# Seven products of quarters for two column groups of the values projection, mixed with the stationary projections, with linear attention behind them

## The chip, the cores and the metric

The kernel runs on one core of one Trainium2 chip. The metric is the device time of one execution in microseconds; the median of several runs is compared. TensorE (PE in the profile) multiplies matrices into PSUM, an accumulator memory of eight banks of 512 float32 columns on 128 partitions. VectorE (DVE) and ScalarE (ACT) do the elementwise work, GpSimd (POOL) and SyncE (SP) mostly issue transfers. Each engine works through its own queue in order; semaphores make one wait for another.

## The reference

Two layers, each on 256 tokens of width 2048. All projections of a layer come from the same input `x` (256 x 2048):

```python
h = x @ w_in                      # a_q, a_k, a_v, a_z, b_q, b_k, b_v, b_z, b_lr, m_q, m_z
y_a = chunk_band_attention(a_q, a_k, a_v, rel_table)     # 8 heads of 128
log_g = log_sigmoid(b_lr @ gate_w + gate_b) / GATE_TAU   # b_lr: 16 columns
o_b = gla_chunk_recurrence(b_q, b_k, b_v, log_g)         # gated linear attention, 4 heads
y_b = rms_norm(o_b) * gla_norm_g
mk, mv = split(mem @ w_mem_kv)
y_m = memory_attention(m_q, mk, mv)                      # 4 heads, 256 memory tokens
y = concat(y_a * silu(a_z), y_b * silu(b_z), y_m * silu(m_z))
x = layer_norm(alpha * x + y @ w_out, ln_g, ln_b)
```

The change touches the values: the product of `x` with the columns of `b_lr`, `b_v` and `a_v`, 16 + 512 + 1024 = 1552 columns in all.

## The kernel before

**Arithmetic.** Every big product is done in three matmuls of a 32-bit format of TensorE: each operand is split into a high part (a cast, on ACT) and a low part (operand minus high part, on DVE), and high x high, low x high and high x low are accumulated. For activations the split is done once and kept (`xq[l]`, four operands of four k tiles each); for weights it is done for each piece as it arrives.

**Weights as a stream of pieces.** `plan()` writes out the order in which all pieces of weights are used (`loads`). A piece is 128 partitions x 1024 columns (512 KB) for most products and 128 x 776 (two k tiles of 388 columns, 388 KB) for the values. `take()` hands out the next piece and lets `advance()` issue what lies ahead of it: the transfer into a ring of four raw tiles (`RAWS`) on SP's queue, the cast three pieces ahead (`high`, line 200, ACT), the low part two pieces ahead (`low`, line 207, DVE). The order of PE and SP is the order in which the program issues; ACT and DVE are put in an order by the scheduler of the framework, where these casts and low parts go first (`tc.high_priority(AHEAD)`).

**Two kinds of projection.** In a stationary projection (`ws_group`) the weights are the stationary operand and the output is transposed, features on partitions; 512 columns of output take two halves of four pieces, each half into two PSUM banks (`pair()` gives banks 0 and 1 or 2 and 3 in turn). In a moving projection (`as_group`) a 128 x 128 block of `x` is stationary and the weights stream through: 388 columns of values in eight pieces of 12 matmuls (two k tiles, two halves of the tokens, three products). `values(i)` does the i-th of four such groups and copies the result into `asv` (tokens on partitions).

**The order in a layer.** Memory keys and values first (16 pieces; in layer 1, `norm_between` prepares that layer's `xq` behind them). Then BQK (linear attention's queries and keys), `values(0)`, `values(1)`, `values(2)`, AQ0, AK0, `values(3)`, AQ1, AK1, MQ, the four gates BZ, AZ0, AZ1, MZ, and the output projection. All but the values and the output are stationary projections of eight pieces.

**Background work by ticks.** Linear attention (`gla`), the attention heads (`a_head`, eight), the memory heads (`m_head`, four), `norm_between` and `norm_residual` are generators that wait in a list. After each piece the program calls `tick()`: at most two generators are active, and at most one of them, in turns, is advanced by one step; the number that it yields says how many ticks it rests. So the few matmuls of a step come into PE's queue between two pieces of a projection, and its DVE and ACT work runs beside the pieces that follow. `banks(n)` takes banks from a list `free` (4 to 7 from `values(2)` on). `gla` needs `values(0)` and `values(1)` (its gates, its values), so it starts at `values(2)`; the heads 0 to 3 are put into the list when `values(2)`, AQ0 and AK0 are done. Where the result of generators is needed, `finish(gens)` calls `tick()` until they are done:

```python
sz = gated()
total(sz, a, b)
act.activation(sz, sz, AF.Silu)
finish(gens[i])
dve.tensor_tensor(yraw[i][:, j:j + 2], sz, yraw[i][:, j:j + 2], op=ALU.mult)
```

This stands at the end of each half of a gate: BZ needs linear attention (`gens[0]`), AZ0 the heads 0 to 3, AZ1 the heads 4 to 7, MZ the memory heads.

Of the kernel before, what the change touches and what calls it, by code (L numbers as in the profile page):

```python
# [16 lines left out]
P = 128  # L17
# [10 lines left out]
VISITS = ((-1, 0), (1, 2), (3, 4), (5,))  # L28

# [7 lines left out]
class Load:  # L37
    def __init__(self, src, shape, home=None, quarter=None):
        self.src, self.shape, self.home, self.quarter = src, shape, home, quarter
        self.raw = self.hi = self.lo = self.room = None  # L40


@with_exitstack
def hybrid_trunk_kernel(
# [81 lines left out]
    xq = [[] for _ in range(L)]  # L126

    def plan():
        for l in range(L):
# [14 lines left out]
            for p in range(8):  # L144
                if l == 0 and p < 4:
                    loads.append(Load(xT[p], (4, T), "res", (xq[l], p)))
                loads.append(Load(w512[l, G_BQK, p], (4, 256)))
            for i in range(4):
                group(w388[l, i], 2, 388)
                for g in ((), (), (G_AQ0, G_AK0), (G_AQ1, G_AK1))[i]:  # L150
                    loads.extend(Load(w512[l, g, p], (4, 256)) for p in range(8))
            for g in (G_MQ, G_BZ, G_AZ0, G_AZ1, G_MZ):
                loads.extend(Load(w512[l, g, p], (4, 256)) for p in range(8))
# [12 lines left out]
    rooms = []  # L166
# [6 lines left out]
    def start_load(d):  # L173
        kp, n = d.shape
        if d.home == "res":
# [13 lines left out]
    def high(d):  # L189
# [9 lines left out]
        with tc.high_priority(AHEAD):  # L199
            act.copy(d.hi, d.raw)  # L200
# [10 lines left out]
    def raws(i):  # L211
        return sum(1 for d in loads[at["lo"]:i] if d.home != "res" and not d.room)

    def advance(hi, lo):
        def dma(upto):
            while at["dma"] < min(upto, len(loads)):
                if loads[at["dma"]].home != "res" and not loads[at["dma"]].room and raws(at["dma"]) >= RAWS:
                    return
                start_load(loads[at["dma"]])
                at["dma"] += 1  # L220
# [83 lines left out]
    def ws_group(l, after=None, first=None):  # L304
        for half in range(2):
            a = pair() if half or first is None else first
            for p in range(4):
# [5 lines left out]
                if p == 3:  # L313
                    v = ps[:, a:a + 2].rearrange("p b (h t) -> p b h t", h=2)
                    yield half * 2, v[:, :, 0], v[:, :, 1]
                tick()

# [38 lines left out]
    def gla_inputs(l):  # L356
        gb = small([P, 2], "gb")
        ng = small([P, 1], "ng")
        raw = small([P, 256], "gws")
# [8 lines left out]
    def gla(gb, ng, gq, gk, asv, yraw):  # L368
# [29 lines left out]
        b_ = hd.tile([P, 512], F32, name=nm("b"), tag="gb_")  # L398
# [28 lines left out]
        qe = hd.tile([P, 512], F32, name=nm("qe"), tag="qe")  # L427
# [217 lines left out]
    def norm_between(x):  # L645
# [13 lines left out]
        for q in range(4):  # L659
            o = operand()  # L660
            x.append(o)
            for j in range(0, 4, 2):
# [10 lines left out]
                parts(o[:, j:j + 2, 0], o[:, j:j + 2, 1], z)  # L673
                yield 2 if (q, j) == (2, 2) else 1

    def norm_residual(rows):
        for n, (g, b) in enumerate(rows):
            for t in range(2):
                r = res[:, t, columns(n)]
                dve.tensor_tensor(r, r, g, op=ALU.mult)  # L680
                dve.tensor_tensor(r, r, b, op=ALU.add)
                yield 1
# [43 lines left out]
    gens, rows = [], None  # L726
    for l in range(L):
# [28 lines left out]
        if l:  # L756
            finish(gens)
            waiting.append(norm_residual(rows))

        yraw = [per.tile([P, 4, T], F32, name=nm("yr"), tag=f"yr{i}") for i in range(4)]  # L760
# [6 lines left out]
        for i, a, b in ws_group(l, None, 4):  # L767
            total(gk if i else gq, a, b, 1.0 if i else 0.125)
        gp = gla_inputs(l)
        if l == 0:  # L770
# [8 lines left out]
            sp.dma_start(res, xn.rearrange("(t p) d -> p t d", p=P))  # L779

        asv = per.tile([P, 2, 1552], F32, name=nm("asv"), tag="asv")

        def values(i):
            for acc in as_group(xq[l], 388):
                act.copy(asv[:, :, i * 388:(i + 1) * 388], acc)

        def heads():
            t = hd.tile([P, 4, T], F32, name=nm("qk"), tag="qk", bufs=4)
            for i, a, b in ws_group(l):
                total(t[:, i:i + 2], a, b)  # L790
            return t

        values(0)
        values(1)
        if l == 0:
            pe.transpose(ps[:, 7, :P], lng, ident)
            act.copy(lnt, ps[:, 7, :32].rearrange("p (a k) -> p a k", a=2))
        free[:] = [4, 5, 6, 7]
        bias = {}
# [4 lines left out]

        load_bias(0)
# [3 lines left out]
        for half in range(2):  # L809
            values(2 + half)  # L810
            q, k = heads(), heads()
            gens.append([a_head(half * 4 + h, load_bias, bias, q[:, h], k[:, h], asv, yraw[1 + half][:, h]) for h in range(4)])
            waiting.extend(gens[-1])
        q = [hd.tile([P, 4, T], F32R, name=nm("mq"), tag="qk", bufs=4) for _ in range(2)]
        for i, a, b in ws_group(l):
            tmp = gated()
            total(tmp, a, b)
            parts(q[0][:, i:i + 2], q[1][:, i:i + 2], tmp)
        gens.append([m_head(h, q, mk, mv, yraw[3][:, h]) for h in range(4)])
# [15 lines left out]
        for i in range(4):  # L835
            for j, a, b in ws_group(l, cut_y if i == 3 else None):
# [10 lines left out]
        rows = gain_rows(l)  # L847
        if last:
            gbrow = per.tile([2, 1024], F32, name="gbrow", tag="yr0")
# [9 lines left out]
        if not last:  # L859
            gens = [norm_between(xq[l + 1])]  # L860
# [112 lines left out]
```

## Time and profile before

| | |
|---|---|
| time, median of 3 runs | 929.47 us (929.41 to 930.95) |
| profiled execution: time and span | 930.37 us, 928.6 us |
| busy: PE, DVE, ACT | 920.9, 592.7, 503.7 us |
| mean granted clock of TensorE | 0.998 |
| moved by DMA | 178.79 MB, 193 GB/s in the mean |
| layer 0: `values(2)` from, `gla`'s last transposes, last memory head's transposes | about 108.5, 200, 344 us |

The busy time of PE counts matmuls, whose ends are modelled; it says that PE has work, not at which rate. Rows of groups read: line, engine, operation, output<-inputs, shape, count | busy time in us, mean ns of one | idle time of the engine before them and what ended it. Rows of the timeline read: start in us, duration in us, engine, line, operation; several like instructions in sequence are one row. A line can be that of a helper: line 77 issues nearly all matmuls, lines 337 and 338 copy an accumulator out, lines 341 and 342 split an activation, 520 to 539 are the end of `gla`, 596 to 610 are in `m_head`, 839 is a gate's SiLU. Rows of stretches read: stretch, its length, busy time of PE, of PE's weight loads, of DVE, ACT and POOL (with counts), granted clock, DMA share, GB/s.

### The profile page before, as it was taken

The page shows a single profiled execution, that of the slowest core. Times are in us where ns is not written, and L with a number is a line of the kernel's source. Part 1 is how long each engine was busy: PE and PEld are TensorE (multiplying, and loading weights), DVE is VectorE, ACT ScalarE, POOL GpSimd, SP SyncE. Part 2 cuts the span into 40 slices and gives each one's busy share as a digit, 9 for nine tenths or more (in the row PEclk, how much of TensorE's full clock was granted, in tenths as well). Part 3 has the DMA queues.
Part 4 walks back from the last instruction along what each step waited for, and adds up shares of the span by engine and source line. Part 5 has one row for each costly group of instructions (what it writes and reads, how often), then busy time and mean ns, then how long its engine had stood idle before and what let it go on. Part 6 is the DMA issues. An engine that isn't in the chain of part 4 may idle for free.

```text
span 928.6 us, 14327 instructions
## 1 busy us (share of the span) xinstructions
PE 920.9 (99%) x5558; PEld 808.5 (87%) x5558; DVE 592.7 (64%) x789; ACT 503.7 (54%) x727; POOL 17.6 (2%) x40
## 2 busy tenths in 40 slices
PE   9999999999999999999999999999999999999997
PEld 6889998898888888888888899889988888888875
DVE  6574497665566666555589544965655666666566
ACT  6563584484456665443468446746644566563340
POOL 2000000000000000000000000000000000100000
PEclk9999999999999999999999999999999999999999
DMA  8867765465645467555665566655655455665552
GB/s 283 291 216 266 213 211 166 149 188 178 196 162 170 170 194 225 195 197 189 201 230 189 171 185 202 186 180 153 201 179 182 163 172 182 216 200 196 190 174 90
DMA packets 58580, 178.79 MB, mean 193 GB/s; under 512 B 6416, under 2 KB 9616, under 8 KB 58256
## 3 DMA queue, kind: packets, MB, share of 16 engines
q1 hardware_dynamic: 56560, 173.05, 57.4%
q0 software_dynamic: 1664, 4.31, 2.0%
q8 instruction: 43, 0.70, 0.3%
q10 hardware_dynamic: 288, 0.52, 0.2%
q14 instruction: 25, 0.20, 0.1%
HBM read 175.76 MB, written 2.10 MB: 192 GB/s over the span
## 4 chain that ended last, share of the span: by engine, by line
PE 96%; DMA 1%; DVE 1%; SPq 1%; issue 0%; ACT 0%; ACTq 0%; DVEq 0%
PE ps L77 95%; DMA raw<-w 1%; DMA room<-w 1%; DVE wl L207 1%; PE ps L572 1%; PE ps L668 0%; PE ps L610 0%; SPq L272 0%; PE ps L539 0%; SPq L267 0%; ACT res L700 0%; DVE w L207 0%; ACT wh L200 0%; PE ps L441 0%; SPq L179 0%
## 5 line engine op out<-in xcount | busy, mean ns | idle before, releaser
L207 DVE TENSOR_TENSOR wl<-raw,wh 128x1024 fp32r<-128x1024 f32 (+1 forms) x313 | 365.7, 1170 | 262.2 <-PE ps L77 207.2
L200 ACT CAST wh<-raw 128x1024 fp32r<-128x1024 f32 (+1 forms) x313 | 314.8, 1007 | 327.4 <-PE ps L77 228.7
L77 PE MATMUL ps<-x,wh 128*128 128x512 f32 x1408 | 448.8, 400 | 0.0
L77 PEld LDWEIGHTS ps<-x,wl 128*128 128x128 f32 x1408 | 264.3, 188 | 63.3 <-DVE wl L207 1.2
L77 PE MATMUL ps<-wh,x 128*128 128x512 f32 (+1 forms) x1112 | 319.0, 368 | 0.1
L77 PE MATMUL ps<-x,wl 128*128 128x256 f32 x1408 | 277.5, 278 | 0.5 <-DVE wl L207 0.5
L77 PEld LDWEIGHTS ps<-wh,x 128*128 128x128 f32 x1112 | 204.2, 188 | 24.3 <-ACT wh L278 1.3
L77 PEld LDWEIGHTS ps<-x,wh 128*128 128x128 f32 x1408 | 216.6, 189 | 2.1 <-ACT wh L200 0.3
L77 PE MATMUL ps<-wl,x 128*128 128x512 f32 (+1 forms) x556 | 204.4, 368 | 0.7 <-DVE wl L207 0.7
L77 PEld LDWEIGHTS ps<-wl,x 128*128 128x128 f32 x556 | 104.5, 188 | 14.8 <-DVE wl L207 1.7
L563 ACT ACTIVATE sc<-sc,mx 128x128 f32<-128x128 f32 (+1 forms) x32 | 14.3, 448 | 19.9 <-DVE mx L561 19.9
L338 DVE SCALAR_TENSOR_TENSOR sz<-ps,sz 128x512 f32<-128x512 f32 x24 | 16.4, 689 | 2.3 <-ACT sz L337 0.3
L632 DVE SCALAR_TENSOR_TENSOR res<-res,ps 128x512 f32<-128x512 f32 x16 | 10.9, 682 | 8.0 <-PE ps L77 8.0
L337 ACT ACTIVATE sz<-ps 128x512 f32<-128x512 f32 x24 | 14.2, 592 | 1.1 <-PE ps L77 1.1
L77 PE MATMUL ps<-w,x 128*128 128x512 f32 (+1 forms) x72 | 14.3, 357 | 0.0
L77 PEld LDWEIGHTS ps<-w,x 128*128 128x128 f32 x72 | 12.0, 189 | 2.2
L841 DVE TENSOR_TENSOR yr<-sz,yr 128x512 f32<-128x512 f32 x16 | 11.0, 687 | 4.2 <-ACT sz L839 4.2
L839 ACT ACTIVATE sz<-sz 128x512 f32<-128x512 f32 x16 | 10.1, 632 | 6.1 <-DVE sz L338 6.0
L77 PE MATMUL ps<-qk,qk 128*128 128x128 f32 (+1 forms) x64 | 13.1, 326 | 0.0
L77 PE MATMUL ps<-sc,asv 128*128 128x256 f32 (+1 forms) x64 | 13.0, 326 | 0.0
L342 DVE TENSOR_TENSOR x<-yr,x 128x512 fp32r<-128x512 f32 x16 | 10.7, 688 | 3.2 <-ACT x L341 3.1
L412 ACT ACTIVATE sc<-sc 128x512 f32<-128x512 f32 x12 | 7.5, 628 | 9.0 <-DVE sc L410 9.0
(173 smaller groups left out, 518.0 us busy)
## 6 DMA issues: line engine op xcount, KB each, us to landing
raw<-w SPq DMA_DIRECT2D x252, 512.0 KB, 3.6
raw<-w SPq DMA_DIRECT2D x64, 388.0 KB, 3.2
bias<-relw SPq DMA_DIRECT2D x16, 192.0 KB, 4.1
res<-xT SPq DMA_DIRECT2D x4, 512.0 KB, 6.2
res<-xn SPq DMA_DIRECT2D x1, 2048.0 KB, 9.0
sc<-ln_g POOLq DMA_DIRECT2D x8, 256.0 KB, 4.4
sc<-ln_b POOLq DMA_DIRECT2D x8, 256.0 KB, 6.3
raw<-memT SPq DMA_DIRECT2D x4, 512.0 KB, 4.5
```

Source lines behind the costliest of these rows:

```text
L77: pe.matmul(o, l, r, start=start, stop=stop, skip_group_check=True)
L200: act.copy(d.hi, d.raw)
L207: dve.tensor_tensor(d.lo, d.raw, d.hi.bitcast(F32), op=ALU.subtract)
L337: act.mul(dst, b, scale)
L338: dve.scalar_tensor_tensor(dst, a, scale, dst, op0=ALU.mult, op1=ALU.add)
L342: dve.tensor_tensor(lo, src, hi.bitcast(F32), op=ALU.subtract)
L412: act.activation(dd, dd, AF.Abs)
L563: act.activation(s[:, own[t]], s[:, own[t]], AF.Exp, bias=mx[:, t:t + 1], accum_out=zs[:, t:t + 1])
L572: pe.transpose(ps[:, pt, i * P:(i + 1) * P], s[:, i * P:(i + 1) * P], ident)
L632: dve.scalar_tensor_tensor(r, r, ALPHA, acc, op0=ALU.mult, op1=ALU.add)
L839: act.activation(sz, sz, AF.Silu)
L841: dve.tensor_tensor(yraw[i][:, j:j + 2], sz, yraw[i][:, j:j + 2], op=ALU.mult)
```

## The change

**Products.** Values' first two column groups (776 columns) are taken as one product of 2 x 2 blocks: `x` in two halves of the tokens and two interleaved halves of the 16 k tiles, the weights in the same halves of k and the two column groups. Instead of eight products of blocks there are seven, after Strassen in Winograd's form. Four products need differences of blocks of `x` (`differences`, split and kept in the tiles of `yraw` and in scratch), and four need sums of blocks of weights, formed by DVE when the pieces have arrived (`high`, with `d.plus`). A block product is done in four quarters of six matmuls of 388 columns (`quarter`). The three products with plain weights come first (`plain_products`: 12 pieces, accumulated in banks 6 and 7), then the four with summed weights (`sum_products`: 16 pieces, banks 4 to 7), and six DVE operations combine the blocks in `asv`.

**Order.** The pieces are mixed one by one with those of stationary projections. After four pieces of BQK, `PART_B` gives 8 wide pieces (W) and 12 plain ones, `PART_A` 16 summed pieces (T) and 16 wide ones; the wide ones are BQK, AQ0, AK0 and half of AQ1. Then come `values(2)`, the rest of AQ1, `values(3)`, AK1, MQ and the gates.

**Background.** `gla` is put into the list behind all of this, as the seven products use banks 4 to 7; the heads 0 to 3 after `values(2)`. `norm_residual` (layer 1) and a new `residual` (layer 0: the load of the residual in four parts) and `norm_vectors` are made active with it.

**Transfers.** The plain pieces are transferred once, and the pieces for the sums once more, into three single tiles and the ring: 28 transfers of 388 KB a layer instead of 16. A transfer into a single tile is issued only when the sums that use its old content have been issued (`d.behind`).

```diff
+PART_B = "WBWBWBWBWBBWBBWBBWBB"
+PART_A = "TW" * 16
...
+            stream = iter([Load(w512[l, g, p], (4, 256)) for g in (G_BQK, G_AQ0, G_AK0, G_AQ1) for p in range(8)][4:])
+            b11, b12, b21, b22 = ([w388[l, n, 2 * q + k] for q in range(4)] for k, n in ((0, 0), (0, 1), (1, 0), (1, 1)))
+            plain = iter([Load(b, (2, 388)) for b in b11 + b22 + b21])
+            loads.extend(next(stream if c == "W" else plain) for c in PART_B)
...
+                    d.parts = [[(0, b11[q]), (1, b12[q])], [(2, b22[q])], [], [(3, b21[q])]][k]
...
+                    d.behind = (sums[n + 2].at, sums[n + 1].at) if d.sum[1] == 0 else (sums[n + 3].at, sums[n + 2].at)
...
         with tc.high_priority(AHEAD):
+            if d.plus is not None:
+                dve.tensor_tensor(d.raw, d.raw, d.plus, op=ALU.add)
             act.copy(d.hi, d.raw)
...
+    def differences(l, q, z0, z1):
+
+        a11, a21, a12, a22 = z0[:, :, :P], z0[:, :, P:], z1[:, :, :P], z1[:, :, P:]
...
+        raw = hd.tile([P, 4, 2, P], F32, name=nm("raw"), tag="qb")
+        dve.tensor_tensor(raw[:, 0], a22, a21, op=ALU.subtract)
+        dve.tensor_tensor(raw[:, 2], a11, raw[:, 0], op=ALU.add)
+        dve.tensor_tensor(raw[:, 3], a12, raw[:, 2], op=ALU.subtract)
+        dve.tensor_tensor(raw[:, 1], a11, a21, op=ALU.subtract)
+        parts(s24[:, 0], s24[:, 1], raw[:, 2:])
+        parts(s1[:, 0], s1[:, 1], raw[:, 0])
+        parts(s3[:, 0], s3[:, 1], raw[:, 1])
...
+    def quarter(o, a, start, stop):
+        wh, wl = take()
+        for kk in range(2):
+            ah, al = (x[:, kk] for x in a)
+            mm(o, ah, wh[:, kk], start and kk == 0, False)
+            mm(o, al, wh[:, kk], False, False)
+            mm(o, ah, wl[:, kk], False, stop and kk == 1)
...
+    def sum_products(l, asv, n1, n2):
+
+        q5, q7, q6, q4 = (ps[:, b, :388] for b in (4, 5, 6, 7))
+        for q in range(4):
+            s1, s2, s3, s4 = diff[l][q]
+            for o, a in ((q5, s1), (q7, s3), (q6, s2), (q4, block(xq[l][q], 1, 1))):
+                quarter(o, a, q == 0, q == 3)
+                if q == 3 and o is q4:
...
+                tick()
+                yield
...
+    def norm_residual(l):
+        for n in range(4):
+            for a, op in ((ln_g, ALU.mult), (ln_b, ALU.add)):
+                row = gated().rearrange("p b t -> p (b t)")
+                pool.dma_start(row, a[l:l + 1, columns(n)].to_broadcast([P, 512]))
+                for t in range(2):
+                    r = res[:, t, columns(n)]
+                    dve.tensor_tensor(r, r, row, op=op)
+            yield 2
...
+        for c in PART_B:
+            run(wide if c == "W" else narrow, 1)
+        narrow = sum_products(l, asv, n1, n2)
...
+        for c in PART_A:
+            run(wide if c == "W" else narrow, 1)
+        yraw = [per.tile([P, 4, T], F32, name=nm("yr"), tag=f"yr{i}") for i in range(4)]
         free[:] = [4, 5, 6, 7]
...
+        gens = [[gla(*gp, gq, gk, asv, yraw[0])]]
         waiting.extend(gens[0])
+        others = [norm_residual(l - 1)] if l else [residual(), norm_vectors()]
+        active.extend((g, now[0] + 1) for g in others)
+        values(2)
+        add_heads(0)
+        run(wide)
+        values(3)
+        run(heads())
+        add_heads(1)
```

More of the change, by code (lines that the diff above doesn't have):

```diff
@@ L673, in norm_between, with norm_vectors @@
                 parts(o[:, j:j + 2, 0], o[:, j:j + 2, 1], z)
+                if j == 0:
+                    z0 = z
+                else:
+                    differences(l, q, z0, z)
                 yield 2 if (q, j) == (2, 2) else 1
[L676 to L682, printed above, removed]
+    def norm_residual(l):
[7 more added lines that the diff above has]
+            yield 2
+    def norm_vectors():
+        pt, = yield from banks(1)
+        pe.transpose(ps[:, pt, :P], lng, ident)
+        act.copy(lnt, ps[:, pt, :32].rearrange("p (a k) -> p a k", a=2))
+        release(pt)
     def last_norm(t, rows, chunks, shared):
```

168 lines of the change are left out of this document (123 added, 45 removed).

## The prediction

> **What bounds the kernel now.** I read the page first (busy shares, then the chain of work that ended last), then the costliest groups of instructions with their shapes kept apart, then the timeline around the places that the change touches.
>
> ```profile
> span 928.6 us, 14327 instructions
> PE 920.9 (99%) x5558; PEld 808.5 (87%) x5558; DVE 592.7 (64%) x789; ACT 503.7 (54%) x727; POOL 17.6 (2%) x40
> PE 96%; DMA 1%; DVE 1%; SPq 1%; issue 0%; ACT 0%; ACTq 0%; DVEq 0%
> ...
> 115.39 0.52 PE L77 MATMUL ps<-wh,x 128*128 128x388 f32 x2
> ...
> 125.98 0.63 PE L77 MATMUL ps<-x,wh 128*128 128x512 f32 x2
> ...
> 137.14 0.60 PE L441 MATMUL ps<-ident,sc 128*128 128x128 f32 x4
> ```
>
> The chain is TensorE (PE) for 96% of the span. So a matmul taken out is worth its cadence, and any microsecond in which PE's in-order queue stands on a wait is paid in full. The last three rows give the cadence. From 115.39 to 125.98 PE does five pieces of values' third column group, 60 matmuls of 388 columns: 10.59 us, 0.1765 us a matmul. From 125.98 to 137.14 it does four pieces of a stationary projection (call one W): 2.79 us each.
>
> **The gain.** Per layer, two column groups are now 2 x 8 pieces x 12 = 192 such matmuls. Seven products of four quarter-pieces of 6 are 168. 24 x 2 layers x 0.1765 = 8.5 us less PE work; nothing else leaves PE.
>
> **Feeding the seven products.** They need 28 weight pieces a layer instead of 16, plus 16 additions of pieces, and each takes only 6 x 0.1765 = 1.06 us of PE.
>
> ```profile
> L207 DVE TENSOR_TENSOR wl<-raw,wh 128x1024 fp32r<-128x1024 f32 x249 | 303.9, 1222 | 194.7 <-PE ps L77 153.6 <-issue 31.1 <-ACT wh L200 6.0
> L200 ACT CAST wh<-raw 128x1024 fp32r<-128x1024 f32 x249 | 260.9, 1049 | 244.0 <-PE ps L77 158.2 <-issue 60.5 <-DMA raw<-w 13.0
> L207 DVE TENSOR_TENSOR wl<-raw,wh 128x776 fp32r<-128x776 f32 x64 | 61.8, 966 | 67.5 <-PE ps L77 53.6 <-issue 5.2 <-ACT wh L200 4.5
> L200 ACT CAST wh<-raw 128x776 fp32r<-128x776 f32 x64 | 53.9, 843 | 83.3 <-PE ps L77 70.5 <-DMA raw<-w 8.9 <-issue 2.5
> L681 DVE TENSOR_TENSOR res<-res,sc 128x512 f32<-128x512 f32 x8 | 5.3, 680 | 0.0
> L680 DVE TENSOR_TENSOR res<-res,sc 128x512 f32<-128x512 f32 x8 | 5.2, 680 | 0.0
> 13.90:46.50 32.60, 32.59 (x166) 27.77 (x167) 20.97 (x18) 18.73 (x19) 0.00 (x0) 1.00 0.87 295
> 478.00:508.00 30.00, 30.00 (x169) 25.77 (x168) 27.45 (x36) 25.14 (x37) 0.64 (x2) 1.00 0.68 229
> ```
>
> The tightest stretch is the 16 pairs of a summed piece and a W. On VectorE (DVE): addition 0.97 (the 128x776 subtraction is the nearest row), low part 0.97, W's low part 1.22 = 3.15 us against 1.06 + 2.79 = 3.85 us of PE. ScalarE (ACT): 0.84 + 1.05 = 1.89. The four copies of the accumulators and six combinations add some 6 us of DVE to 62. It fits at 91%, with the weights prepared two to three pieces ahead. Transfers: 16 x 0.524 + 16 x 0.397 MB in 61.6 us = 239 GB/s, and 8 x 0.524 + 12 x 0.397 in the 35 us of plain products = 256 GB/s. Row 13.90:46.50 has 295 GB/s with PE busy 32.59 of 32.60 us (last columns: clock, DMA share, GB/s). The terms are single tiles whose next transfer waits until their sums are used (the waiting issue also holds later weights behind it on SP's queue), but they come free nearly seven pieces before they are needed again, some 9 us. I take 0; the bounds are 0 and 4 us a layer.
>
> The differences of the activations cost, per quarter, four 256-column subtractions and 1,024 columns of splits on DVE, about 3.1 us, 12.6 us a layer. In layer 1 they fall into a stretch where DVE has 27.45 of 30 us; but the residual's scale and shift, 8 x 0.68 twice = 10.9 us there, move behind the products. DVE nets +1.7, ACT about +5 on 25.14 of 30. I take +1 us; bounds 0 and 4. In layer 0 DVE has room behind the memory stage: 0. The residual's load in four parts, its rows through POOL and the LayerNorm vectors' transpose have 8 to 20 us to spare: 0.
>
> **What moves: the background work has too few pieces left.** This is the large term. Linear attention and the heads are generators; one step of one of them is issued per piece of projection (a tick), two of them taking turns. Linear attention's 22 steps start today at values' third group, and 59 ticks pass until the first gate needs its output; the heads join only after 24 of these. After the change it starts after the mixed pieces, two and a half projections later: values' third group 8, rest of AQ1 4, values' fourth 8, AK1 8, MQ 8, BZ 3 = 39 ticks. In these it shares turns with the residual's four steps and, behind that, with heads 0, 1 and 2, four steps each, and the start of head 3. Played through by the yields, `finish(gens[0])` in the middle of BZ must force 7 steps in layer 0 and 5 in layer 1 back to back, and `finish(gens[3])` in the middle of MZ forces 8 in each (memory heads 2 and 3). Today no step is forced. A forced step puts its matmuls into PE's queue ahead of the gate's second half with no piece between, so PE stands for the DVE/ACT chain that the pieces cover now. The first chain, today:
>
> ```profile
> 183.69 1.10 PE L77 MATMUL ps<-asv,pairs 64*64 64x128 f32 x32
> 184.62 1.05 PE L77 MATMUL ps<-st,qe 64*64 64x128 f32 x24
> 185.60 0.62 PE L77 MATMUL ps<-wh,x 128*128 128x388 f32 x2
> ...
> 184.85 2.27 ACT L520 COPY sc<-ps 64x512 f32<-64x512 f32 x4 [0.25 <-PE ps L77]
> 187.27 0.31 ACT L527 ACTIVATE sq<-sc 128x128 f32<-128x128 f32 x1 [0.15 <-DVE sc L523]
> ...
> 191.94 0.18 ACT L527 ACTIVATION_READ_ACCUMULATOR sq<-sc 128x1 f32 x1
> 192.15 1.28 ACT L347 ACT_TABLE_LOAD   x1
> 193.44 0.30 ACT L347 ACTIVATE rs_u<-ms,eps 128x8 f32<-128x8 f32 x1
> ...
> 195.63 1.29 DVE L533 TENSOR_TENSOR sc<-sc,rr 128x512 f32<-128x512 f32 x2
> ...
> 200.08 1.03 PE L539 MATMUL ps<-ident,sc 128*128 128x128 f32 x8
> ```
>
> Output matmuls end at 185.60, the scaled rows at 196.92: 11.3 us. Two casts (1.9 us) stand among the eight squares and one low part (1.2) ahead of the scaling. Without these: rest of the copies 1.5 (to 187.12), squares 4.85 - 1.9 = 3.0, table and root 1.6, small DVE steps 1.9 - 1.2 = 0.7, scaling 1.3 = 8.1. PE waits for it before the transposes of L539. In layer 0 the output matmuls are themselves forced, so only head 3's transposes and products (0.7 us) lie beside: 8.1 - 0.7 = 7.4 to 11.3 - 0.7 + 2 (the gate's SiLU and its table load among the squares) = 12.6; I take 10, as few weights can be cast while PE stands. In layer 1 they are issued two pieces earlier: 5.6 us less, 1.8 to 7; I take 5. The second chain:
>
> ```profile
> 327.76 0.88 PE L77 MATMUL ps<-mk,mq 128*128 128x256 f32 x6
> 331.26 0.88 PE L77 MATMUL ps<-mk,mq 128*128 128x256 f32 x6
> 340.34 0.60 PE L610 MATMUL ps<-ident,sc 128*128 128x128 f32 x4
> ...
> 330.07 1.28 ACT L600 ACT_TABLE_LOAD   x1 [1.24 <-DVE mx L597]
> 340.42 0.63 ACT L839 ACTIVATE sz<-sz 128x512 f32<-128x512 f32 x1
> 341.89 0.58 ACT L341 CAST sc<-ps 128x512 fp32r<-128x512 f32 x1
> ...
> 336.35 0.62 DVE L605 TENSOR_SCALAR sc<-sc,zs 128x256 f32<-128x256 f32 x2
> ...
> 342.50 0.69 DVE L342 TENSOR_TENSOR sc<-ps,sc 128x512 fp32r<-128x512 f32 x1
> ```
>
> Memory head 3's scores end at 332.14, its scaled rows at 336.97: 4.8 us (3.8 without a cast and a low part). From the start of the transposes (340.34) to the split rows (343.19) another 2.9, of which a gate in between takes 1; bare 0.6 + 0.58 + 0.69 = 1.9. In MZ, head 3's scores come right behind the piece, so the chain is 0.9 + 4.8 + 1.9 + 0.9 (products, as long as the scores) = 8.5 us with some 3.2 us of PE's own work in it (scores, two times transposes and products, overlapping): 5.3. Floor 4.3 without the cast and low part; with SiLU and a second table load between, 8.5. I take 6 in each layer.
>
> **The clock behind a stall.**
>
> ```profile
> 1.51 3.78 PE L77 MATMUL ps<-wh 128*128 128x512 f32 x8 [1.51 <-DVE wh L248]
> 922.14 1.98 PE L77 MATMUL ps<-gbrow,row 2*128 2x512 f32 x4 [0.34 <-ACT row L696]
> 924.00:925.00 1.00, 0.12 (x1) 0.00 (x0) 0.00 (x0) 0.57 (x1) 0.00 (x0) 0.54 0.58 217
> ```
>
> The first eight 512-column matmuls start 0.45 us apart (1.51 to 5.09) against 0.23 later, and as PE runs out at 924 the granted clock is 0.54. So a stall of several microseconds probably leaves about 3.6 us at half speed, 1.8 us lost. Bounds: 0 and 4 x 1.8 = 7.2; I take two of four, 3.6. The Trainium skill ("TensorE: Matmul & The Clock Gate", Part 1) says that an idle window of about 3.4 us halves the clock and a busy one brings it back; by it the term would be an estimated 6.8, all four stalls being longer. The two ends of this trace agree in direction; none has a stall in its middle.
>
> One more rule speaks against the change. The Trainium skill ("ScalarE: Activation LUTs", What ACT_TABLE_LOAD costs) puts a change of function set at 1.28 us and a drain of 1.38. Here the load takes 1.28 and the root starts 0.01 us behind it (192.15, 193.44), so I count 1.28; by that section each of the four stalls would be an estimated 1.4 longer.
>
> **Sum.** -8.5 + 10 + 5 + 2 x 6 + 3.6 + 1 = +23.1 us. The profiled execution took 930.37 us with its span of 928.6; the median of the three runs is 929.47, 0.9 less. 930.4 + 23.1 - 0.9 = 952.6; I say 952.
>
> **Rivals.**
> 1. Faster: the forced steps find their operands ready, the four stalls together stay under 8.5 us (about 2 each), and the time is 921 to 928. For it: weights stop competing while PE stands. Against it: the barest first chain is 8.1 us and nothing can lie beside it in layer 0. It decides only if the steps are not forced, that is if my count of ticks is wrong.
> 2. The stalls at their floors and no loss of clock: 7.4 + 1.8 + 8.6 - 8.5 + 1 for the differences = +10.3: 940. For it: ACT and DVE have little else to do then.
> 3. The mixed region is fed too slowly. DVE is the bound if the pair's 3.15 us passes 3.85; each 0.3 us beyond costs 32 x 0.3 = 10 us: 962. For it: 91% on an in-order engine, single tiles for the terms. Against it: rows of 0.97 us that hardly vary, and 295 GB/s without a stall.
> 4. The gain is not there, the quarter products running at a worse cadence: 961. Each is as wide as before and changes its stationary operand as often, so this is unlikely.
> 5. The clock falls behind all four stalls: 7.2 instead of 3.6, 956. For it: at the end the small matmuls from 922.14 on, under 2 us of them, were quiet enough for the clock to fall by 924.5; the shortest stall is longer.
>
> **How the numbers follow.** Forecast (943 to 956 about 952) 0.45; rival 5 (953 to 961) 0.18; rival 2 (936 to 943) 0.16; rivals 3 and 4 (957 to 975) 0.14; rival 1 0.07, of which 0.02 end within 0.2% of 929.5, which is about what a measurement of this kernel can tell from no change. The range 937 to 962 leaves out rival 1, a little of rival 2 and most of rival 3. Faster 0.05, same 0.02, slower 0.93.
>
> **What would show it.** Matmuls of 388 columns fall from 768 to 720, and the mixed region runs PE without gaps at 1.06 and 2.79 us. PE is idle ahead of L539's transposes in the middle of BZ (about 10 us in layer 0, 5 in layer 1) and ahead of L610's and the products behind them in the middle of MZ (about 6 in each), released by DVE and ACT; the granted clock falls behind the longest. If PE stays 99% busy, the count of ticks was wrong; if the gaps lie in the products instead, the feeding was.

## The result and the profile after

The changed kernel takes 970.53 us (median of 4 runs, 968.28 to 971.37) against 929.44 us before on the same chip: ratio 1.0434 (1.0413 to 1.0456). It is slower, as forecast, but by 41 us where the forecast's sum has 23 (952, range 937 to 962). A second set of runs on another chip gave 969.18 against 930.43, ratio 1.0417 (1.0403 to 1.0432). The profiled execution took 971.11 us with a span of 969.3.

The page of the kernel after: span, PE's busy time, PE and its granted clock in 40 slices, and the chain of work that ended last.

```profile
span 969.3 us, 14487 instructions
...
PE 925.7 (95%) x5510; PEld 809.0 (83%) x5510; DVE 663.2 (68%) x913; ACT 553.9 (57%) x795; POOL 17.7 (2%) x40
...
PE   8999999999959997999999899999999899979997
...
PEclk9999999999979998999999999999999999989999
...
PE 78%; DMA 7%; DVE 6%; ACT 4%; issue 3%; SPq 1%; ACTq 0%; DVEq 0%
```

PE has 48 matmuls less (5510 against 5558), as counted, but is 95% busy instead of 99%, and the chain now leaves PE for a fifth of the span. The row of PE dips at slices 12, 16 and 36, and less at 23 and 32. The row of the clock dips at 12, 16 and 36; the shorter falls show in finer stretches (below).

PE's timeline at the four forced places, where each row ends with the idle time before it and what ended it:

```profile
278.43 0.55 PE L687 MATMUL ps<-ident,sc 128*128 128x128 f32 x3 [1.19 <-ACT sc L635]
282.12 1.65 PE L82 MATMUL ps<-sc,asv 128*128 128x256 f32 x4 [3.15 <-ACT sc L689]
289.60 1.97 PE L654 MATMUL ps<-ident,sc 128*128 128x128 f32 x8 [5.83 <-DVE sc L648]
...
373.93 0.72 PE L725 MATMUL ps<-ident,sc 128*128 128x128 f32 x4 [2.39 <-DVE sc L720]
378.97 1.09 PE L725 MATMUL ps<-ident,sc 128*128 128x128 f32 x4 [4.33 <-DVE sc L720]
...
764.48 1.02 PE L82 MATMUL ps<-sc,asv 128*128 128x256 f32 x4 [3.20 <-ACT sc L689]
765.74 1.97 PE L654 MATMUL ps<-ident,sc 128*128 128x128 f32 x8 [0.24 <-DVE sc L648]
...
848.92 0.72 PE L725 MATMUL ps<-ident,sc 128*128 128x128 f32 x4 [2.04 <-DVE sc L720]
853.96 1.09 PE L725 MATMUL ps<-ident,sc 128*128 128x128 f32 x4 [4.32 <-DVE sc L720]
```

These are the stalls of the forecast, at the places it named: 10.2 us in the middle of BZ in layer 0, 3.4 in layer 1, 6.7 and 6.4 in the two MZ. Together 26.7 us, where 27 were taken. What ACT and DVE do in the first stall and in the MZ of layer 0:

```profile
277.21 2.25 ACT L635 COPY sc<-ps 64x512 f32<-64x512 f32 x4
279.48 1.28 ACT L994 ACT_TABLE_LOAD   x1
280.78 0.63 ACT L994 ACTIVATE sz<-sz 128x512 f32<-128x512 f32 x1
...
286.39 1.28 ACT L462 ACT_TABLE_LOAD   x1
287.68 0.30 ACT L462 ACTIVATE rs_u<-ms,eps 128x8 f32<-128x8 f32 x1
...
288.85 1.29 DVE L648 TENSOR_TENSOR sc<-sc,rr 128x512 f32<-128x512 f32 x2
...
373.63 1.28 ACT L994 ACT_TABLE_LOAD   x1
375.27 0.63 ACT L994 ACTIVATE sz<-sz 128x512 f32<-128x512 f32 x1 [0.36 <-DVE sz L453]
375.92 1.28 ACT L715 ACT_TABLE_LOAD   x1
```

The chain is the expected one: copies, squares, root, scaling. The gate's SiLU stands among them with its table load, and in MZ the exponential needs its table back, which is the case that the forecast held for its upper end (8.5 us). The root starts 0.01 us behind its load and the SiLU of the first stall 0.02 us behind its own. The Trainium skill ("ScalarE: Activation LUTs", What ACT_TABLE_LOAD costs) counts another 1.38 for a drain; no row here shows it, and the measurement decides.

The clock behind the stalls, in stretches (PE busy is the second figure behind the stretch, the clock the third from the end):

```profile
281.00:294.00 13.00, 6.05 (x21) 5.22 (x22) 3.74 (x10) 9.19 (x30) 0.55 (x1) 0.50 0.00 0
377.00:382.00 5.00, 3.03 (x14) 3.04 (x15) 2.07 (x5) 2.66 (x8) 0.00 (x0) 0.50 0.01 3
550.00:553.00 3.00, 2.62 (x8) 2.43 (x9) 3.00 (x5) 0.53 (x1) 0.32 (x2) 0.52 0.64 114
764.00:768.00 4.00, 3.28 (x15) 2.94 (x16) 2.25 (x6) 3.69 (x8) 0.00 (x0) 0.64 0.00 0
854.00:857.00 3.00, 3.00 (x14) 2.98 (x15) 1.36 (x3) 0.96 (x2) 1.13 (x3) 0.50 0.05 10
```

The clock falls behind all four, not two. PE busy times (1 - clock) is 3.0 + 1.5 + 1.3 + 1.2 + 1.5 = 8.5 us in these rows; over the whole span, in stretches of 1 us, it is 9.9. Some of that lies between the gaps of a stall (the four matmuls from 282.12 take 1.65 us, and PE then waits for DVE anyway), so it is the upper end of what the clock cost in time.

The third row, at 550, is behind a gap that the forecast did not have. PE, DVE and the DVE waits in layer 1's mixed region:

```profile
550.38 0.69 PE L82 MATMUL ps<-wl,x 128*128 128x388 f32 x1 [2.55 <-DVE wl L242]
567.49 0.50 PE L82 MATMUL ps<-x,wl 128*128 128x256 f32 x2 [1.31 <-DVE wl L242]
...
542.33 1.29 DVE L802 TENSOR_TENSOR res<-res,sz 128x512 f32<-128x512 f32 x2 [2.38 <-DMA sz<-ln_g]
...
548.16 1.29 DVE L802 TENSOR_TENSOR res<-res,sz 128x512 f32<-128x512 f32 x2 [1.59 <-DMA sz<-ln_g]
549.37 2.10 DVE L242 TENSOR_TENSOR wl<-raw,wh 128x776 fp32r<-128x776 f32 x2
...
DVE res L802 <- DMA sz<-ln_g: 6.2, 4, 2.4
```

Line 802 is the residual's scale and shift. In the program it is issued behind the products; on DVE it runs inside them, at 542 to 566, because the scheduler may draw it forward. Each time it reaches a row of `ln_g` that has not landed, DVE stands, and the low parts of the weights stand behind it: PE waits for line 242. With the smaller gaps at 582 to 586 this region has 5.4 us of PE gaps in layer 1; one of 0.6 of them stays when scale and shift are left out (below).

All PE gaps together are 38.3 us after and 3.2 before. The account of the two profiled executions (+40.7 us):

| term | forecast | measured |
|---|---|---|
| 48 matmuls of 388 columns less | -8.5 | -8.5 (count and cadence) |
| forced steps: BZ, layers 0 and 1; MZ, both | 10 + 5 + 12 | 10.2 + 3.4 + 13.1 |
| clock (PE busy at half speed, halved) | 3.6 | 9.9 |
| gaps in layer 1's mixed region (residual's scale and shift) | 0 | 5.4 |
| differences, feeding, other gaps | 1 | 3.0 |
| not assigned to a gap or to the clock | | 4.3 |
| sum | 23.1 | 40.7 |

Most of what is not assigned is busy time of PE: it grew by 4.8 us (925.7 against 920.9), where 48 matmuls less and the clock make -8.5 + 9.9 = 1.4.

### The profile page after: what moved, and what is told of

The parts are those of the page before. It is cut to its first block, busy times and chain, and to the rows that moved or that the text cites. A ratio compares the mean times of both kernels' runs of the same rounds, so it can differ in the third digit from the quotient of the medians.

```text
span 969.3 us, 14487 instructions
## 1 busy us (share of the span) xinstructions
PE 925.7 (95%) x5510; PEld 809.0 (83%) x5510; DVE 663.2 (68%) x913; ACT 553.9 (57%) x795; POOL 17.7 (2%) x40
## 4 chain that ended last, share of the span: by engine, by line
PE 78%; DMA 7%; DVE 6%; ACT 4%; issue 3%; SPq 1%; ACTq 0%; DVEq 0%
PE ps L82 76%; DVE wl L242 3%; DMA raw<-w 2%; DMA term<-w 2%; DMA sz<-ln_g 1%; ACT wh L235 1%; DMA sz<-ln_b 1%; DMA room<-w 1%; ACT sq L642 1%; DMA raw<-memT 1%; PE ps L687 0%; PE ps L654 0%; PE ps L725 0%; ACT L715 0%; ACT sc L635 0%
## 5 line engine op out<-in xcount | busy, mean ns | idle before, releaser
L82 PE MATMUL ps<-wh,x 128*128 128x512 f32 (+1 forms) x952 | 278.3, 374 | 0.4 <-ACT wh L319 0.4
L82 PEld LDWEIGHTS ps<-wh,x 128*128 128x128 f32 x952 | 174.7, 189 | 23.8 <-ACT wh L319 1.0
L82 PE MATMUL ps<-wl,x 128*128 128x512 f32 (+1 forms) x476 | 177.8, 374 | 4.6 <-DVE wl L242 4.6
L82 PEld LDWEIGHTS ps<-wl,x 128*128 128x128 f32 x476 | 89.9, 189 | 18.1 <-DVE wl L242 5.8
L234 DVE TENSOR_TENSOR term<-term,term 128x776 f32<-128x776 f32 x24 | 23.1, 964 | 12.8 <-DMA term<-w 12.4
L235 ACT CAST wh<-term 128x776 fp32r<-128x776 f32 x24 | 20.2, 841 | 12.3 <-DVE term L234 10.9
L242 DVE TENSOR_TENSOR wl<-term,wh 128x776 fp32r<-128x776 f32 x24 | 23.0, 960 | 2.0 <-ACT wh L235 2.0
L725 PE MATMUL ps<-ident,sc 128*128 128x128 f32 x32 | 6.0, 316 | 13.1 <-DVE sc L720 13.1
L82 PEld LDWEIGHTS ps<-sc,asv 128*128 128x128 f32 x64 | 11.5, 197 | 7.8 <-ACT sc L689 6.8
L82 PE MATMUL ps<-wh,sc 128*128 128x388 f32 x64 | 16.5, 339 | 0.6 <-ACT wh L235 0.6
L82 PE MATMUL ps<-wh,s 128*128 128x388 f32 x64 | 16.5, 339 | 0.0
L747 DVE SCALAR_TENSOR_TENSOR res<-res,ps 128x512 f32<-128x512 f32 x16 | 10.9, 683 | 7.9 <-PE ps L82 7.9
```

Source lines behind the costliest of these rows:

```text
L82: pe.matmul(o, l, r, start=start, stop=stop, skip_group_check=True)
L234: dve.tensor_tensor(d.raw, d.raw, d.plus, op=ALU.add)
L242: dve.tensor_tensor(d.lo, d.raw, d.hi.bitcast(F32), op=ALU.subtract)
L725: pe.transpose(ps[:, pt, m * 256 + t * P:m * 256 + (t + 1) * P], s[:, t, m * P:(m + 1) * P], ident)
L747: dve.scalar_tensor_tensor(r, r, ALPHA, acc, op0=ALU.mult, op1=ALU.add)
```

## The experiments

The theory going in: the forced steps and the clock behind them cost most of it, and the early residual the rest. The rivals: the seven products themselves are slow (fed too slowly), or the gain isn't there.

**Two steps per tick.** A tick advances up to two steps, so that no step is left for `finish` to force.

```diff
+        steps = 0
         while True:
...
                 active.append((g, now[0] + after))
-                return
+                steps += 1
+                if steps == 2:
+                    return
+                continue
```

> The changed kernel with up to two steps of the background work in a tick instead of one; counted by the yields, no step is forced in either layer. Theory (forced steps): the idle time of PE ahead of the transposes of linear attention's and the memory heads' ends (10.2, 3.5, 6.7 and 6.4 us in the changed kernel's trace) goes, and with it the stretches at half clock behind them (about 10 us): 970.5 - 27 - 10 = 934 us, 930 to 940. Rival (the mixed pieces and their feeding are what costs): at most 10 us less, 960 us or more.

Measured: 932.93 us against 930.42, ratio 1.0031 (1.0019 to 1.0043), clock 0.997. All four stalls are gone, and 37.6 us with them: 26.7 of them idle time of PE; the clock is part of the rest (PE busy at half speed, halved, is 1.5 us instead of 9.9). What stays is the layer-1 region (rows of PE, then of DVE's waits):

```profile
528.11 0.69 PE L82 MATMUL ps<-wl,x 128*128 128x388 f32 x1 [2.61 <-DVE wl L246]
545.21 0.39 PE L82 MATMUL ps<-x,wl 128*128 128x256 f32 x1 [1.63 <-DVE wl L246]
...
DVE res L806 <- DMA sz<-ln_g: 5.6, 4, 2.4
```

So DVE's waits for the residual's rows come before these gaps without any forced step too; that the residual causes them is shown only by leaving it out (below).

**Fillers in the forced steps.** Useless matmuls (4 to 20, into a bank that is written afterwards) stand where PE would be idle, to keep the clock up. The steps stay forced.

```diff
         pt, = yield from banks(1)
+        fill(pt, 9 if h == 2 else 17)
         for m in range(2):
             for t in range(2):
                 pe.transpose(
```

> The changed kernel with matmuls of 512 columns without use put into the forced steps, each lot a little shorter than the gap at its place (4, 12, 20 in layer 0's BZ, 4 and 12 in layer 1's, 9 and 17 in both MZ). No wait gets shorter. Theory (PE works at half clock behind each stall): the granted clock stays at 1.00 there and the time falls by what the half clock cost, 6 to 10 us: 960 to 965 us. Rival (the lower clock shows in the records only while PE has nothing to do): 970 to 973 us.

Measured: 966.89, ratio 1.0394 (1.0377 to 1.0412), clock 0.997 instead of 0.981. It lies above the expected 960 to 965 and below the rival's 970. It is 3.6 us below the changed kernel, and 2.3 below its second set of runs (4.6 and 2.3 if each is taken against the kernel before on its own chip). The traces say the same by stretches, from the transposes that end a stall to the next landmark: behind BZ in both layers to memory head 3's scores, behind MZ to layer 1's first transposes and to the last small matmuls. They are 2.0, 1.2, 0.8 and 1.9 us shorter than in the first profile of the changed kernel, 5.9 together, and 4.3 shorter than in its second. Of this 1.0 and 0.5 are smaller gaps in the last stretch, so that 4.9 and 3.8 are left for the clock. The stalls themselves take as long as without fillers (13.7 us instead of 13.4 in the first BZ, 8.2 instead of 8.3 in the first MZ): the chain on ACT and DVE sets them. So half clock cost 2 to 5 us of time behind the four stalls; the rest of its 9.9 lies in the stalls and behind the gap at 548, and what that is worth in time was not tried.

**Rows in another tile.** The residual's rows use the tile of the weight terms, which comes free only behind the sums, so that DVE can't meet them in the products.

```diff
-                row = gated().rearrange("p b t -> p (b t)")
+                row = hd.tile([P, 2, 388], F32, name=nm("row"), tag="term").rearrange("p k n -> p (k n)")[:, :512]
```

> The changed kernel with the rows of the residual's scale and shift in the tile of the third weight term, which is in use until the summed products are over, so that their transfers and the multiplications that wait for them can't be drawn forward into the plain products of layer 1. Theory (drawn forward, VectorE stands for the rows and the low parts of weights come late): PE's gaps at 547 to 550 and 566 to 586 us go (5.4 us idle, about 2 us at half clock): 962 to 966 us. Rival (the weights' transfers are what is late there, as 263 to 294 GB/s are moved): 969 to 972 us.

Measured: 968.13, ratio 1.0401 (1.0376 to 1.0425). In the trace layer 1 is 7.5 us shorter from the last transposed residual to linear attention's first transposes, but 4.4 us longer from there to the next head's transposes (PE gaps of 1.52 at 657 and 2.44 at 673). The expected 962 to 966 was missed: the wait moved.

**Both of these edits with two steps per tick, and the fillers with late rows.**

> Two steps in a tick and the residual's rows in the term's tile. Theory: both gains add, 970.5 - 37 - 6 = 927 us, 923 to 932: the seven products then bring some of their 8.5 us. Rival (differences and summed pieces keep DVE and the transfers too busy): 935 us or more.

> The changed kernel with both the matmuls without use in the forced steps and the residual's rows in the term's tile. Theory (half clock behind the four stalls and the early wait for the rows costs some 8 to 10 us, and the rows' new place gives 2 to 3): 10 to 12 us below the changed kernel of the same chip. Rival (the half clock costs less than 4): 4 to 7 us below.

Two steps and late rows: 932.55, ratio 1.0017 (1.0006 to 1.0027), no better than two steps alone within the intervals; both the expected 927 and the rival's 935 were missed. Fillers and late rows: 966.63, ratio 1.0388 (1.0374 to 1.0402), no better than the fillers alone, and 2.5 us below the changed kernel on its chip where 10 to 12, or 4 to 7, were expected. Neither place of the residual's work was free. The second one also showed how short a gap brings the clock down (below).

**The changed kernel once more,** beside the next runs on their chip.

> The changed kernel once more, for comparison on the same chip: 968 to 972 us.

969.18 (above). Its stalls are those of the first profile within 0.3 us; PE busy at half speed, halved, is 6.9 us in that execution, against 9.9.

**Scale and shift left out.** Two steps per tick, and an empty generator stands in for `norm_residual`, so layer 1's residual is neither scaled nor shifted.

```diff
-        others = [norm_residual(l - 1)] if l else [residual(), norm_vectors()]
+        others = [iter(())] if l else [residual(), norm_vectors()]
```

> Two steps in a tick; the residual's scale and shift between the layers are left out (no rows, 16 VectorE operations of 0.68 us less). It bounds what their place can be worth. Theory (they are what is late in layer 1): 925 us, 922 to 928. Rival (the weights' transfers and the differences are): 930 us or more.

Measured: 926.95, ratio 0.9961 (0.9948 to 0.9973). With two steps per tick the price of the scale and shift is 932.93 - 926.95 = 6.0 us, whatever its mechanism. With one step per tick no run leaves them out.

**At the end of the list.** Two steps, rows in the tiles of linear attention's queries and keys, the generator behind the memory heads.

```diff
+                row = hd.tile([P, 2, T], F32, name=nm("row"), tag="gq" if a is ln_g else "gk")...
...
+        if l:
+            waiting.extend(others)
```

> Two steps in a tick; in layer 1 the residual's scale and shift come last in the list, behind the memory heads, with their rows in the tiles of linear attention's queries and keys, which are free only when that is over. Theory (with no forced step left, VectorE's waits for the residual's rows and the low parts behind them are the largest part of what is lost): 926 us, 923 to 929, so faster than the kernel before, as 8.5 us of products are saved and some 4 to 5 us of small gaps stay. Rival (the summed pieces and the differences take what the products save): 930 to 933 us.

Measured: 934.23, ratio 1.0042 (1.0028 to 1.0056). It failed: the operations were drawn forward again, to 682 to 702, where DVE stood 5.6 us for rows with linear attention's pairs behind them; PE had gaps of 1.53 and 4.42 us there.

**On GpSimd.** The eight pairs of operations by `pool.tensor_tensor`, in the changed kernel and with two steps.

```diff
-                    dve.tensor_tensor(r, r, row, op=op)
+                    pool.tensor_tensor(r, r, row, op=op)
```

> The changed kernel with the residual's 16 multiplications and additions of layer 1 on GpSimd, whose queue holds the rows' transfers, instead of VectorE. Theory (VectorE standing for the rows is the whole loss in layer 1's mixed region, 8.5 us from the first transposed residual to linear attention's first step, and nothing comes back later because GpSimd has no other work): 8 us below the changed kernel, 961 us, 958 to 964. Rival (the transfers and the differences take part): 965 us or more.

> Two steps in a tick and the residual's scale and shift on GpSimd. Theory (both large losses gone): as without the scale and shift, 927 us, 925 to 929, so 0.2 to 0.5% faster than the kernel before. Rival (GpSimd's work slows VectorE, whose operations then come late in the mixed region and beside linear attention): 931 us or more.

Measured: 972.43, ratio 1.0440 (1.0423 to 1.0458), and 938.87, ratio 1.0086 (1.0071 to 1.0101). Both theories missed. With one step the time is that of the changed kernel within the intervals; with two steps, moving the work off DVE cost some 5 us. From the run with two steps, the groups of low parts at 500 to 570 us, while GpSimd works, GpSimd's operations and a row of DVE:

```profile
L246 DVE TENSOR_TENSOR wl<-raw,wh 128x1024 fp32r<-128x1024 f32 x15 | 21.5, 1432 | 2.2 <-PE ps L82 1.0 <-issue 0.7 <-ACT wh L239 0.2
L246 DVE TENSOR_TENSOR wl<-raw,wh 128x776 fp32r<-128x776 f32 x12 | 13.8, 1162 | 11.1 <-ACT wh L239 7.6 <-PE ps L82 3.1 <-issue 0.2
...
L806 POOL TENSOR_TENSOR res<-res,sz 128x512 f32<-128x512 f32 x16 | 26.3, 1670 | 18.8 <-PE ps L82 10.1 <-DMA sz<-ln_g 6.3 <-DMA raw<-w 2.5
...
524.65 3.62 DVE L246 TENSOR_TENSOR wl<-raw,wh 128x776 fp32r<-128x776 f32 x2 [0.60 <-PE ps L82]
```

The groups' means were 1222 and 966 ns in the kernel before. In this trace the eight low parts that lie for over half of their time beside an operation of GpSimd take 1.00 to 2.05 us (776 columns) and 1.99 to 2.31 (1024), all that lie beside none 0.95 to 0.97 and 1.20 to 1.23. That this alone makes the 5 us was not separated.

**Rows requested ahead, operations queued behind a low part.** The rows are requested one step early, and the operations are put behind the last low part issued before them, so that DVE can't reach them before that. With two steps per tick and with one.

```diff
-                for t in range(2):
-                    r = res[:, t, columns(n)]
-                    dve.tensor_tensor(r, r, row, op=op)
-            yield 2
+                rows.append(row)
+            yield 3
+            with tc.issue_after(last_low[0]):
+                for row, op in zip(rows, (ALU.mult, ALU.add)):
+                    for t in range(2):
+                        r = res[:, t, columns(n)]
+                        dve.tensor_tensor(r, r, row, op=op)
```

> Two steps per tick, and the residual's rows are requested a step ahead of their eight pairs of operations, which are queued on DVE behind the last low part issued before them, so that DVE can't reach them before their rows are there. If the residual's cost is DVE standing for rows (2.60 + 1.64 + 0.73 us of PE gaps in the run with two steps alone, 7 us between the residual left out and kept), the time falls to that of the run with scale and shift left out, 927, plus at most 2 us: 927 to 929, ratio 0.996 to 0.999, and DVE has no wait of over 1 us for a row. If it is the 10.9 us of DVE work itself, beside linear attention, that costs, it stays at 932 to 934.

> The same edit of the residual, with one step per tick as in the changed kernel. If the residual's operations, drawn forward into the mixed products, cost some 8 us of PE gaps there and nothing gives them back, 961 to 964. If the gain is given back in linear attention, as in the runs with late rows and with GpSimd, 967 to 970: what then stands is the forced steps' chain, whose start doesn't come earlier when the products end earlier.

Measured: with two steps 932.89, ratio 1.0026 (1.0017 to 1.0035); with one 970.01, ratio 1.0433 (1.0414 to 1.0452). No DVE wait for a row is left, the mixed region of layer 1 has gaps of only 0.38 and 0.58 us with two steps, and yet nothing is won. In the first, two gaps have come up behind the products (PE's rows, then a stretch of this kernel with PE busy first and DVE busy third, then the same stretch with scale and shift left out):

```profile
646.80 0.69 PE L82 MATMUL ps<-sc,sc 64*64 64x64 f32 x32 [1.59 <-DVE sc L539]
659.86 0.30 PE L691 MATMUL ps<-ident,sc 128*128 128x128 f32 x1 [3.05 <-DVE sc L686]
...
640.00:660.00 20.00, 15.37 (x145) 14.09 (x143) 20.00 (x37) 9.11 (x16) 1.08 (x2) 1.00 0.65 190
```

```profile
640.00:660.00 20.00, 20.00 (x233) 18.81 (x232) 17.12 (x34) 12.71 (x25) 0.00 (x0) 1.00 0.63 196
```

Beside linear attention DVE is busy 17.1 of 20 us without the residual; with 10.9 us more within 29 us (623 to 652) it is full. So waits for rows are one way to pay, and the work itself in a full stretch is the other. In the kernel with one step per tick the residual's steps now rest three ticks instead of two, and linear attention's turns fall otherwise: played through by the yields, 7 steps are forced in layer 1's BZ instead of 5.

```profile
755.57 0.55 PE L687 MATMUL ps<-ident,sc 128*128 128x128 f32 x3 [0.81 <-ACT sc L635]
758.97 1.65 PE L82 MATMUL ps<-sc,asv 128*128 128x256 f32 x4 [2.85 <-ACT sc L689]
765.85 1.54 PE L654 MATMUL ps<-ident,sc 128*128 128x128 f32 x6 [5.24 <-DVE sc L648]
```

PE's gaps there are 8.9 us instead of 3.4: what was won in the products is lost again.

**The same, among the gates.** Two steps, rows requested ahead, operations queued behind a low part, and the generator behind the memory heads with its rows in the tiles of linear attention's queries and keys.

```diff
+                row = hd.tile([P, 2, T], F32, name=nm("row"), tag="gq" if a is ln_g else "gk")...
...
+            with tc.issue_after(last_low[0]):
...
+        if l:
+            waiting.extend(others)
```

> Two steps per tick, the residual's operations queued behind a low part as in the run before, and moved behind the memory heads in the list of layer 1, with the rows in the tiles of linear attention's queries and keys: they should lie among the gates, where DVE has some 38 of 60 us busy. If the residual costs only where DVE is full (20.00 of 20 us at 640 to 660 in the run before), the time is that of the run without scale and shift, 926.95, plus at most 1.5: 926.5 to 928.5, ratio 0.996 to 0.998, and no PE gap of over 1 us behind 100 us. If 10.9 us more of DVE cost wherever they lie, 932 to 934.

Measured: 927.00 us against 930.67, ratio 0.9964 (0.9951 to 0.9976): the time of the kernel without scale and shift, with the work done, and 0.4% faster than before the change. Its page, and a stretch of it among the gates, where the operations now lie; then the same stretch before the change:

```profile
span 924.6 us, 14484 instructions
...
PE 912.9 (99%) x5510; PEld 800.4 (87%) x5510; DVE 661.9 (72%) x913; ACT 535.1 (58%) x781; POOL 17.7 (2%) x40
...
PEclk9999999999999999999999999999999999999999
...
800.00:860.00 60.00, 60.00 (x300) 50.80 (x299) 43.64 (x51) 28.94 (x35) 2.15 (x4) 1.00 0.69 217
```

```profile
800.00:860.00 60.00, 60.00 (x311) 51.23 (x310) 37.16 (x40) 29.85 (x37) 2.66 (x5) 1.00 0.63 210
```

6.5 us more of DVE fit into 60 us and PE stays at 60.00. The sum closes too: 48 matmuls less (-8.5), PE gaps of 6.9 instead of 3.2 (+3.7), no loss of clock: -4.8, and the span fell by 4.0. PE's busy time fell by 8.0 us, from 920.9 to 912.9. The expected "no gap of over 1 us" held but for one of 1.31 us at 893, in the output projection, where the kernel before has 0.50.

## Why the prediction was half right

- **The count of ticks and the forced steps: right.** They are forced where it said, their idle time sums to 26.7 us against 27, released by the named lines, and two steps per tick removed them. Layer 1's BZ came out at 3.4 for 5, MZ at 6.5 each for 6.
- **The gain of 8.5 us: right,** as far as the last kernel can tell: PE's busy time is 8.0 us less, and the sum closes to 0.8 us with the gain in it. The rival that the quarter products run at a worse cadence falls.
- **Feeding and differences: right in the mixed region.** The rival of a mixed region fed too slowly falls: without the residual's operations layer 1's mixed region has one gap of 0.58 us. Over the whole kernel small gaps stay: 6.2 us of them in that run, some 3 more than before, where 1 was taken.
- **"I take two of four, 3.6": the step was wrong, and the size came near by luck.** The clock fell behind all four stalls, and in one of the two profiles behind the gap at 548 too. Rival 5 (7.2) had this mechanism, and so had the estimate of 6.8 that the prediction works out from the Trainium skill ("TensorE: Matmul & The Clock Gate", Part 1). In time the four falls cost 2 to 5 us by the run with fillers, so 0.5 to 1.3 each for 1.8: more falls at a lower price make nearly the same sum. The forecast halved the count although its last quoted rows showed that less than 2 us of quiet at the end were enough.
- **"The residual's scale and shift move behind the products": wrong.** That is the order of the program, not that of DVE. The step was costed at nothing, and as a relief of 10.9 us for DVE in the products. It cost 6.0 us (two steps with and without it), as waits for rows in the products or as too much DVE work behind them, and nothing only where both were avoided.

The runs divide the miss, each taken against the kernel before on its chip: the changed kernel +38.8 and +41.1 us (two sets), with two steps +2.5, without scale and shift -3.5. So the forced steps with all that hangs on them cost 36 to 39 us, where the forecast had 27 + 3.6; the residual cost 6.0, where it had 0; and the rest is -3.5, where it had -8.5 + 1. These are 6 to 8, 6.0 and 4.0 us of the 16 to 18 that were missed. Of the 36 to 39, 26.7 are idle time and 2 to 5 the clock behind the stalls; what makes up the rest stays open. Rival 5 alone (956) would still have been 14 us short.

## What to carry to other kernels

When work that runs in the background of a stream is moved later, count the steps that are left for it: what isn't spread over the stream is paid at the next point that needs its result, as the whole bare chain, and a fallen clock adds to it (2 to 5 us behind four such stops here). Where a framework orders an engine's queue, a place in the program is only the earliest place: request data a step ahead, queue its users behind an instruction that belongs there, and choose a stretch in which that engine has room. A lost gain is found by leaving the suspect out altogether first (6.0 us here), and then by trying places for it.

## What the runs showed of the hardware

How long PE must be idle for the clock to fall is not one figure. In the run with fillers and late rows it fell behind 1.80 us, between dense matmuls (PE's rows); in the run with late rows alone it held behind 2.44 us.

```profile
659.42 0.66 PE L82 MATMUL ps<-x,wl 128*128 128x256 f32 x2 [1.80 <-DVE wl L252]
659.88 1.05 PE L82 MATMUL ps<-x,wh 128*128 128x512 f32 x2
```

A pair of 512-column matmuls takes 1.05 us there for 0.63. The clock is 0.50 from 659.60 to 663.01 (below): 3.4 us at half speed, about 1.7 lost.

What sets the two apart is where the idle time lies. The stretches at half speed begin on a grid: in the first profile of the changed kernel at 280.47, 376.04, 550.12, 765.16 and 850.49 us, which lie 28, 51, 63 and 25 times 3.413 us apart, and they last one, two or four times as long (3.41, 6.83, 13.65). Cut by the grid of each trace, the stretches in question read (fillers and late rows, two; late rows; changed kernel, first and second profile):

```profile
656.19:659.60 3.41, 1.61 (x10) 1.08 (x9) 3.41 (x5) 3.38 (x4) 0.54 (x1) 1.00 0.20 57
659.60:663.01 3.41, 3.41 (x12) 2.92 (x13) 3.41 (x7) 3.37 (x6) 0.00 (x0) 0.50 0.55 163
...
671.46:674.87 3.41, 1.75 (x10) 1.44 (x9) 3.07 (x7) 2.91 (x8) 0.00 (x0) 1.00 0.67 224
...
546.71:550.12 3.41, 1.12 (x7) 0.71 (x5) 1.96 (x3) 0.63 (x1) 0.46 (x2) 1.00 0.66 232
...
544.46:547.88 3.42, 1.76 (x11) 1.26 (x9) 1.93 (x4) 0.17 (x2) 0.54 (x1) 1.00 0.78 254
```

PE is busy for 0.47 of the stretch that holds the 1.80 us, and for 0.51 of the one that holds most of the 2.44. The gap at 548 of the changed kernel is 2.55 us in one execution and 2.50 in the other; the first has a stretch busy for 0.33, and the clock falls, the second one of 0.51, and it holds. Over all 15 traces, from 10 us to 8 us before the end, each of the 29 such stretches at full speed in which PE was busy for at most 0.47 was followed by half speed, and none of the others, all busy for 0.51 or more. Full speed came back behind stretches of 0.80 or more, and behind none of 0.79 or less. In the last microseconds, where PE's matmuls have two rows, the clock falls behind busier stretches too.

The Trainium skill ("TensorE: Matmul & The Clock Gate", Part 1) gives an idle window of about 3.4 us, free-running. The grid agrees with that length, and its place differs between two executions of one kernel; that an idle time of half of it can be enough does not follow from the Trainium skill, and the measurement decides here.

An elementwise operation on GpSimd slowed DVE's low parts in the mean from 1.22 to 1.43 and from 0.97 to 1.16 us, single ones to 2.31 and 2.05. The Trainium skill ("SBUF — State Buffer", SBUF: two separate sides) says that the two engines share a pair of ports under a lock when DVE reads two inputs from SBUF and GpSimd reads it too; both do here, and the trace agrees in direction.
